# Modulation blocks released every 14000 of the planner's units instead of 4000, with 43 shared buffers and a 4096-byte scratch for dynamic DMA

## The chip, the core and the metric

The kernel runs on one core of a Trainium2 chip. The metric is the device time of one execution in microseconds (us). Work is spread over TensorE (PE, with its weight loads on PEld), VectorE (DVE), ScalarE (ACT), GpSimd (POOL), and the DMA queues, most of them issued from SyncE (SP). A measurement of this kernel spreads by about 0.1% either way, so a difference of 0.2% (6 us) is about the least that can be told from none.

## The reference

Two blocks on 1024 tokens and 256 context tokens, width 1024, all in float32:

```python
def hybrid_layer(x, xc, c_act, cc_act, w_mod, b_mod, w_in, ...):   # two layers
    shift, scale, gate = jnp.split(c_act @ w_mod + b_mod, 3, axis=-1)
    h = x * (1 + scale[:, None]) + shift[:, None]
    rk, rv, nk, nv, rq, rg, nq, ng, ch, cb, ccg, cz = split_cols(h @ w_in, PROJ_SPLITS)
    mod_c = jnp.split(cc_act @ w_mod[:, :n_mod * D_MODEL] + b_mod[:n_mod * D_MODEL], n_mod)
    hc = xc * (1 + mod_c[1]) + mod_c[0]          # the context, projected in the same way
    y_conv = short_conv_branch(...)              # 4 groups
    y_ret, yc_ret = retention_branch(...)        # 6 heads, chunks of 128, both directions
    y_na, yc_na = neighbourhood_branch(...)      # 6 heads, softmax over an 8x16 window and the context
    y = jnp.concatenate([y_conv, y_ret, y_na], axis=-1) @ w_out
    return layer_norm(ALPHA * x + gate[:, None] * y, ln_g, ln_b), ...
```

The second block takes the result through a gated delta rule (4 heads of 128, chunks of 64) beside dilated attention (8 heads of 64, three patterns), an output projection, and a gated feed-forward part of 2816 columns. What matters here is the first line of each layer: shift, scale and gate are products of one activated vector (c, and one of the context) with the 1024 x 3072 matrix `w_mod` of that layer. They depend on no token, so they can be computed at any time before the layer that uses them; the layer 1 values are not wanted before layer 0 has ended.

## The kernel before, in words

**Arithmetic.** A float32 operand is split into a high and a low part, and a projection is three matmuls, `xl*wh`, `xh*wh` and `xh*wl`, of 128 x 128 weights and up to 512 columns into one of 8 PSUM banks (`pb`). ScalarE makes `wh` and GpSimd makes `wl` from each loaded weight tile.

**Stages.** In the profiled execution: hidden states of layer 0 to 62 us; the V projection to 132; the retention pairs of layer 0 to 345; its conv, neighbourhood-attention (NA) and gate parts to 690; its output and layer norm to 865; layer 1 the same way to 1545 (V to 930, retention to 1110, then conv, NA and gates); the second block's V to 1605; the delta rule and the projections beside it to 1800; dilated attention to 2205; output to 2320; feed-forward to 2745; its last product to 3012.

**What sets the order.** TensorE runs its instructions in the order in which the Python emits them (`tc.manual_schedule`). That order comes from a planner, the class `Mixer`. It keeps a clock of its own, `vt`, and a list `active` of generators (softmax chains, retention chains, the modulation blocks), each with a due time. When a projection's matmul is emitted, `pe()` moves the clock and lets due generators take a step, so that their small matmuls are woven between projections: this text calls that **woven**. Two helpers do otherwise: `run_until(cond)` steps the generators one after the other, with no projection between, until `cond` holds. These stretches are called **forced** here. DVE, ACT, POOL and SP instructions are placed by priority, and the priority is the planner's time (`rank`); those of the modulation blocks get 5000 added (`late=X_MOD`).

**What sets a forced stretch off.** All large tiles come from one pool "S" of `NS` buffers of 4 KB per partition. `room()` counts free buffers, less what each active generator may still take: the larger of zero and its `peak` less what it holds. `S()` (an allocation outside a generator) forces steps until `room() >= 1 - over` with `over` = 2, `need_room(n)` until `room() >= n`, `need_o` and `need2` until a named pair is done. So a generator that stays alive holds room back from everything else.

**The modulation blocks.** `mods_gen` computes 32 blocks of 128 outputs: the last 8 of layer 0 and the 24 of layer 1 (the first 16 of layer 0 are done ahead, in the first stage). Per block it takes a buffer `wm`, loads 512 KB, yields, has DVE multiply and reduce it against `crow` (one or two reductions, named `mjk` and `wm` by where they write, each with a sum `macc`), makes `mod`, frees `wm`, and yields 4000. While it lives it holds the two `crow` buffers and `mjk`, and has a `peak` of 2 on top. It is added right after the hidden states, before the V projection.

**Order of the parts.** `ORDER1` is `r0 r1 r2 c0 n0 c1 n1 g0 g1 n2 g2 g3 g4 g5` in layer 0: three retention pairs, conv groups, NA pairs, gates. `ret_blocks`, `conv_blocks` and `gate_block` all allocate with `S()`; `n` is preceded by `need_room(9)`. The software DMA queue, issued by POOL, is used only at the start of each of the 6 NA pairs, for 11 transfers each (8 of them `nvr`).

Of the kernel before, what the change touches and what calls it, by code (L numbers as in the profile page):

```python
# [26 lines left out]
class Mixer:  # L27
# [7 lines left out]
    def __init__(self):  # L35
# [11 lines left out]
        self.banks = {}  # L47
        self.slots = [0.0] * Base.NS
        self.held = {}
# [213 lines left out]
class Base:  # L263
# [26 lines left out]
        self.uid += 1  # L290
        return f"{s}_{self.uid}"

    NS = 40
    OVER = {}
    NCS = 15

    def S(self, name, shape=(128, 1024), dt=F32):
# [4 lines left out]
        if self.mix.owner is None:  # L302
            self.mix.run_until(lambda: self.mix.room() >= 1 - self.mix.over)
        t = self.pm.tile(list(shape), dt, tag="S", bufs=self.NS, name=self.nm(name))
        self.mix.new_slot(self.mix.key(t))
# [177 lines left out]
class Layers(Base):  # L483
    X_RET = (1500, 1500)
    AHEAD = 3
    STEPS = 2
    X_MOD = 5000.0


    def setup(self):  # L490
# [54 lines left out]
    def mod_gen(self, l, blocks):  # L545
        for b in blocks:
            w = self.S("wm")
            self.nc.sync.dma_start(out=w, in_=self.io["w_modT"][l, b])
            yield
            self.mod_block(l, b, w, 1 if l == 1 and b >= 16 else 2)  # L550
            self.free(w)
            yield 4000
        if l:
            self.free(*self.crow, self.mjk)

# [1053 lines left out]
    def block1(self, stop=None):  # L1609
# [16 lines left out]
        def ready_k(k):  # L1626
            while steps[0] <= min(k + self.STEPS, 7):
                next(h0, None)
                steps[0] += 1
                if steps[0] == 8:  # L1630
                    mix.ratio = 10.0
                    mix.add(self.mods_gen(), True, peak=2, late=self.X_MOD)

# [1062 lines left out]
```

## Time and profile before

| | us |
|---|---|
| median of 3 runs (3010.87 to 3014.09) | 3012.46 |
| the profiled execution | 3013.66 |
| its span | 3011.9 |
| TensorE busy | 2734.6 (91%) |
| VectorE busy | 1986.3 (66%) |
| ScalarE / GpSimd busy | 1185.1 (39%) / 1168.4 (39%) |
| mean granted TensorE clock | 0.952 of full speed |

TensorE is the engine that decides: it is busy for 91% of the span, and the time it is not busy, with the time that it runs below its full clock, is what the order of the work can change. A stretch gives busy time and count per engine, the granted clock as a share of the full 2.4 GHz, the share of the DMA engines and GB/s. A row of waits says which engine and operation TensorE waited for, the total, the count and the longest.

### The profile page before, as it was taken

To read this page: it belongs to the slowest core of one execution; us is meant where nothing else is said; L and a number is where in the kernel's file an instruction comes from. 1 tells how busy PE (TensorE), PEld (TensorE's weight loads), DVE (VectorE), ACT (ScalarE), POOL (GpSimd) and SP (SyncE) were. 2 spreads that over 40 slices of the span, in tenths; PEclk is the share of its full clock that TensorE was granted. 3 is DMA by queue.
4 is the path that set the end of the run, shared out by engine and by line. 5 is a ranking of instruction groups with operands and counts; after the bars stand their busy time and mean duration, and the time that the engine had idled before them with its cause. 6 is when DMAs were issued, how large, how long until landed. Compare 5 with 4: busy or idle time off the path is not lost. (4 is left out here: it accounts for less than half of the span.)

```text
span 3011.9 us, 41163 instructions
## 1 busy us (share of the span) xinstructions
PE 2734.6 (91%) x14508; PEld 2339.8 (78%) x14508; DVE 1986.3 (66%) x3880; ACT 1185.1 (39%) x2691; POOL 1168.4 (39%) x998
## 2 busy tenths in 40 slices
PE   7989999999989989999889968898888899999888
PEld 6977888888778768887787767777767688888666
DVE  6666675684641567665555887777645777776786
ACT  5212254553442125554343323455544333334333
POOL 3345512213443451222563322111145644445755
PEclk9989999999989999999999979899999999999899
DMA  7533212225333221224444343221353222227244
GB/s 255 184 107 98 98 31 80 81 80 194 116 100 103 54 69 36 94 80 154 159 129 143 131 149 109 79 78 53 118 181 108 87 80 80 81 80 283 74 158 157
DMA packets 160975, 341.13 MB, mean 113 GB/s; under 512 B 28704, under 2 KB 56640, under 8 KB 160768
## 3 DMA queue, kind: packets, MB, share of 16 engines
q1 hardware_dynamic: 147968, 316.33, 31.1%
q10 hardware_dynamic: 10016, 13.12, 1.8%
q0 software_dynamic: 2784, 9.05, 1.0%
q8 instruction: 115, 1.88, 0.3%
q14 instruction: 92, 0.75, 0.1%
HBM read 265.46 MB, written 66.67 MB: 110 GB/s over the span
## 5 line engine op out<-in xcount | busy, mean ns | idle before, releaser
L251 POOL TENSOR_TENSOR wl<-wr,wh 128x512 fp32r<-128x512 f32 (+2 forms) x344 | 460.8, 1344 | 1142.3 <-ACT wh L251 1065.7
L344 PE MATMUL pb<-xh,wl 128*128 128x512 f32 x1456 | 579.9, 398 | 1.8 <-POOL wl L251 1.7
L344 PE MATMUL pb<-xh,wh 128*128 128x512 f32 x1456 | 578.9, 398 | 0.0
L344 PE MATMUL pb<-xl,wh 128*128 128x512 f32 x1456 | 578.4, 397 | 0.0
L251 ACT ACTIVATE wh<-wr 128x512 fp32r<-128x512 f32 (+2 forms) x344 | 203.0, 592 | 430.0 <-PE pb L344 328.2
L344 PEld LDWEIGHTS pb<-xh,wl 128*128 128x128 f32 x1456 | 277.4, 191 | 58.3 <-POOL wl L251 3.0
L344 PEld LDWEIGHTS pb<-xh,wh 128*128 128x128 f32 x1456 | 278.0, 191 | 53.4 <-issue 0.3
L344 PEld LDWEIGHTS pb<-xl,wh 128*128 128x128 f32 x1456 | 277.2, 190 | 54.0 <-issue 0.3
L344 PE MATMUL pb<-wh,yhl 128*128 128x512 f32 x832 | 266.4, 399 | 14.1 <-DVE xl L251 4.9
L344 PE MATMUL pb<-T,wh 128*128 128x512 f32 x640 | 198.1, 391 | 11.7 <-DVE T L251 10.4
L344 PEld LDWEIGHTS pb<-wh,yhl 128*128 128x128 f32 x832 | 159.7, 192 | 50.7 <-issue 8.0
L251 POOL TENSOR_TENSOR wl<-ws,wh 128x512 fp32r<-128x512 f32 x100 | 136.2, 1362 | 137.4 <-ACT wh L251 136.3
L344 PE MATMUL pb<-whi,yhl 128*128 128x512 f32 x528 | 174.5, 410 | 14.1 <-DVE yhl L251 6.1
L251 DVE TENSOR_TENSOR yhl<-yr,yhl 128x512 fp32r<-128x512 f32 (+4 forms) x122 | 116.4, 978 | 97.5 <-ACT yhl L251 93.6
L344 PE MATMUL pb<-wl,yhl 128*128 128x512 f32 x416 | 165.7, 398 | 7.3 <-POOL wl L251 7.3
L251 ACT ACTIVATE pt<-pb 128x512 fp32r<-128x512 f32 (+3 forms) x230 | 114.7, 527 | 122.9 <-PE pb L349 120.7
L251 DVE TENSOR_TENSOR pt<-pb,pt 128x512 fp32r<-128x512 f32 (+3 forms) x230 | 129.4, 596 | 49.7 <-ACT pt L251 49.0
L344 PEld LDWEIGHTS pb<-T,wh 128*128 128x128 f32 x640 | 120.5, 189 | 37.5 <-DVE T L251 10.9
L344 PEld LDWEIGHTS pb<-whi,yhl 128*128 128x128 f32 x528 | 104.9, 199 | 40.7 <-ACT whi L251 7.4
L344 PE MATMUL pb<-wl,xh 128*128 128x384 f32 (+1 forms) x384 | 127.4, 332 | 6.5 <-POOL wl L251 6.5
L251 ACT ACTIVATE wh<-ws 128x512 fp32r<-128x512 f32 x100 | 63.2, 632 | 169.8 <-PE pb L344 168.2
L344 PE MATMUL pb<-wh,xl 128*128 128x384 f32 (+1 forms) x384 | 126.4, 329 | 3.8 <-ACT wh L251 1.4
(435 smaller groups left out, 6188.7 us busy)
## 6 DMA issues: line engine op xcount, KB each, us to landing
wr<-in_w_in_dram SPq DMA_DIRECT2D x152, 256.0 KB, 2.7
ws<-in_w_down_dram SPq DMA_DIRECT2D x110, 256.0 KB, 3.8
wr<-in_w_out_dram SPq DMA_DIRECT2D x96, 256.0 KB, 2.9
wm<-in_w_modT_dram SPq DMA_DIRECT2D x32, 512.0 KB, 4.2
wr<-in_w_v_dram SPq DMA_DIRECT2D x64, 192.0 KB, 2.4
ws<-in_w_gate_dram SPq DMA_DIRECT2D x22, 512.0 KB, 5.2
ws<-in_w_up_dram SPq DMA_DIRECT2D x22, 512.0 KB, 4.8
ffn<-F SPq DMA_DIRECT2D x22, 512.0 KB, 3.0
```

The lines of the kernel that those rows point to most:

```text
L251: return fn(*a, **kw)
L344: self.mix.product(c / 2.4, out, (lhsT, rhs), lambda: self.nc.tensor.matmul(out, lhsT, rhs, start=start, stop=stop))
```

## The change

Three numbers: `NS` goes from 40 to 43, the modulation generator yields 14000 instead of 4000 after each block, and the compiled program reserves 4096 bytes for dynamic-DMA scratch, where the default stood before.

```diff
-    NS = 40
+    NS = 43
@@ class Layers
+    MOD_STEP = 14000.0
@@ def mod_gen
             self.mod_block(l, b, w, 1 if l == 1 and b >= 16 else 2)
             self.free(w)
-            yield 4000
+            yield self.MOD_STEP
@@ def kernel
-    nc = _bacc.Bacc("TRN2", target_bir_lowering=False, num_devices=1)
+    nc = _bacc.Bacc("TRN2", target_bir_lowering=False, num_devices=1, dynamic_dma_scratch_size=4096)
```

No instruction is added or taken away on TensorE (11891 rows in both orders). Through the planner the order changes in layer 0 between the first retention pair and the end of the third NA pair, at the end of the last but one NA pair of layer 1, and in the dilated stage. The scratch size alone leaves the order as it was.

First place: TensorE, the first retention pair. `vwc`, `vw`, `ktc`, `kt`, `q` and `k` are retention tiles, `xl`/`xh`/`wl`/`wh` a projection. Before:

```order
L344 MATMUL pb_1746<-ch_367,wh_1636 128x256
L344 MATMUL pb_1746<-ch_367,wl_1637 128x256
L344 MATMUL pb_1799<-vwc_1731,ktc_1716 64x128 x2
L344 MATMUL pb_1799<-vwc_1732,ktc_1716 64x128 x2
L344 MATMUL pb_1804<-vw_1721,kt_1703 64x128 x8
L344 MATMUL pb_1813<-vw_1726,kt_1703 64x128 x8
L344 MATMUL pb_1847<-q_1317,k_1316 128x128
L344 MATMUL pb_1848<-q_1317,k_1316 128x128
```

After, at the same row:

```order
L344 MATMUL pb_1696<-ch_367,wh_1588 128x256
L344 MATMUL pb_1696<-ch_367,wl_1589 128x256
L344 MATMUL pb_1738<-xl_189,wh_1594 128x512
L344 MATMUL pb_1738<-xh_187,wh_1594 128x512
L344 MATMUL pb_1738<-xh_187,wl_1595 128x512
L344 MATMUL pb_1738<-xl_189,wh_1594 128x512
```

The whole forced stretch of that pair (60 rows, the products of `vw`, `q`, `k`, `St`, `rv` and the transposes) is gone; its matmuls now stand woven among the projections that follow.

Second place: TensorE, the first NA pair of layer 0, at the end of its score products `kc*qc`; `sl` and `sc` are the softmax's rows, transposed through `ident`, and `pt`, `nv` the transposed weights and the values. Before:

```order
L344 MATMUL pb_3643<-kc_684_3333,qc_703_3452 128x256
L344 MATMUL pb_3643<-kc_684_3333,qc_705_3454 128x256
L344 MATMUL pb_3583<-xh_251,wh_3468 128x512
L344 MATMUL pb_3583<-xh_251,wl_3469 128x512
L344 MATMUL pb_3583<-xl_253,wh_3468 128x512
L344 MATMUL pb_3583<-xh_251,wh_3468 128x512
```

After:

```order
L344 MATMUL pb_3533<-kc_650_3239,qc_670_3360 128x256
L344 MATMUL pb_3533<-kc_650_3239,qc_672_3362 128x256
L349 MATMUL pb_3569<-ident,sl_3483 128x128 x4
L349 MATMUL pb_3577<-ident,sc_3484 128x128
L349 MATMUL pb_3577<-ident,sc_3485 128x128
L349 MATMUL pb_3577<-ident,sc_3484 128x128
```

Where projections stood between scores and transposes, the transposes now follow at once. The three NA pairs of layer 0 have such stretches of 150, 150 and 97 matmuls without a projection; before, the longest in them were 71 and 35.

Third place: TensorE in the dilated stage, where `dsl` is a softmax row and `dv` a value. Before:

```order
L349 MATMUL pb_19996<-ident,dsl_19887 128x128
L349 MATMUL pb_19996<-ident,dsl_19888 128x128
L344 MATMUL pb_20004<-pt_19962,dv_19857 128x256 x4
L344 MATMUL pb_20004<-pt_19969,dv_19857 128x256 x2
L344 MATMUL pb_20004<-pt_19969,dv_19857 128x128 x2
L344 MATMUL pb_20017<-pt_19977,dv_19857 128x256 x4
```

After, in the same part of the program:

```order
L344 MATMUL pb_20000<-xh_14758,wh_19604 128x512
L349 MATMUL pb_20019<-ident,dsl_19878 128x128
L349 MATMUL pb_20019<-ident,dsl_19879 128x128
L349 MATMUL pb_20019<-ident,dsl_19878 128x128
L349 MATMUL pb_20019<-ident,dsl_19879 128x128
L349 MATMUL pb_20027<-ident,dsl_19878 128x128
```

Before, this stage has stretches without projections of 276, 96, 116 and 96 matmuls. After, it has one of 279 and one of 88 at its end, and between them none longer than 30. On VectorE the 32 modulation blocks, all ahead of the first NA softmax before, are spread out: 16 of them now stand behind that softmax, 5 of these within the three long NA stretches (two, two and one).

## Rows read from the trace of the kernel before

**Rows 1.** The page: span and busy time of each engine.

```profile
span 3011.9 us, 41163 instructions
PE 2734.6 (91%) x14508; PEld 2339.8 (78%) x14508; DVE 1986.3 (66%) x3880; ACT 1185.1 (39%) x2691; POOL 1168.4 (39%) x998
```

**Rows 2.** Busy time by stage: stretch, length, engines (count), clock, DMA share, GB/s.

```profile
62.00:132.00 70.00, 66.82 (x372) 65.73 (x372) 52.15 (x99) 21.62 (x68) 34.34 (x26) 0.95 0.52 165
132.00:345.00 213.00, 194.15 (x1203) 165.54 (x1202) 147.11 (x357) 37.90 (x74) 108.30 (x96) 0.92 0.37 110
345.00:515.00 170.00, 167.59 (x989) 147.37 (x988) 105.64 (x270) 80.04 (x212) 49.14 (x59) 1.00 0.21 69
515.00:690.00 175.00, 166.06 (x1025) 149.09 (x1024) 126.97 (x349) 96.11 (x265) 26.94 (x29) 0.96 0.28 93
1800.00:2205.00 405.00, 351.63 (x2142) 301.91 (x2141) 292.26 (x782) 201.94 (x483) 65.35 (x58) 0.95 0.28 93
```

**Rows 3.** The same view: first retention pair, then woven retention of a later pair.

```profile
200.00:233.30 33.30, 21.09 (x161) 18.63 (x160) 31.14 (x71) 4.61 (x9) 18.62 (x17) 0.64 0.39 105
...
319.90:322.30 2.40, 2.40 (x42) 2.23 (x41) 2.40 (x4) 0.39 (x1) 1.28 (x3) 1.00 0.96 333
328.50:336.20 7.70, 7.70 (x76) 6.46 (x76) 6.80 (x22) 0.00 (x0) 1.73 (x4) 1.00 0.00 0
```

**Rows 4.** TensorE's waits from 200 to 233.3 us: total, times, longest.

```profile
PE pb L349 <- DVE k L251: 6.0, 1, 6.0
PE pb L344 <- DVE St L251: 4.9, 1, 4.9
```

**Rows 5.** Stretches: woven parts of the first NA pair of layer 0.

```profile
390.80:394.10 3.30, 3.16 (x22) 2.94 (x22) 2.14 (x7) 1.80 (x5) 1.04 (x1) 1.00 0.42 159
405.80:412.70 6.90, 6.90 (x58) 6.90 (x57) 4.95 (x12) 3.32 (x9) 1.28 (x1) 1.00 0.00 0
426.90:430.50 3.60, 3.60 (x28) 3.56 (x28) 2.51 (x9) 0.76 (x2) 0.00 (x0) 1.00 0.10 36
```

**Rows 6.** Stretches: forced NA parts, two of layer 0 and one of layer 1.

```profile
552.10:568.20 16.10, 11.32 (x74) 10.03 (x73) 14.22 (x33) 8.32 (x22) 9.65 (x14) 0.79 0.35 109
668.60:681.50 12.90, 9.08 (x54) 8.47 (x53) 9.43 (x25) 4.43 (x9) 2.38 (x2) 0.74 0.62 203
...
1269.00:1295.60 26.60, 19.50 (x117) 17.51 (x116) 21.98 (x57) 15.70 (x46) 10.92 (x15) 0.81 0.27 87
```

**Rows 7.** TensorE's waits from 1269 to 1295.6 us.

```profile
PE pb L349 <- DVE sl L251: 6.3, 4, 2.7
```

**Rows 8.** Tiles of the modulation blocks: ns min/median/max, first and last start.

```profile
L251 DVE CUSTOM_DVE_ANT_0 mjk<-wm,crow x24: 1204/1224/2332, 67.2 to 269.6; 128x1024 f32<-128x1024 f32 x24
...
L251 SPq DMA_DIRECT2D wm<-in_w_modT_dram x32: 327/384/702, 61.1 to 321.1; - x32
L251 DVE CUSTOM_DVE_ANT_0 wm<-wm,crow x32: 1208/1224/2306, 69.6 to 340.8; 128x1024 f32<-128x1024 f32 x32
...
L251 DVE TENSOR_SCALAR mod<-macc,bmod x40: 201/223/1310, 22.1 to 342.3; 128x2 f32<-128x2 f32 x32, 128x1 f32<-128x1 f32 x8
```

**Rows 9.** Stretches: three forced parts of the dilated stage.

```profile
2008.60:2027.20 18.60, 13.66 (x98) 11.87 (x97) 17.15 (x59) 12.21 (x28) 1.30 (x1) 1.00 0.18 54
2060.80:2089.70 28.90, 20.11 (x117) 17.81 (x118) 27.24 (x84) 17.04 (x37) 1.59 (x2) 0.88 0.08 26
2139.20:2159.90 20.70, 15.05 (x97) 13.16 (x98) 17.80 (x56) 12.26 (x29) 1.02 (x1) 0.92 0.30 95
```

**Rows 10.** TensorE's waits from 2060.8 to 2089.7 us.

```profile
PE pb L344 <- ACT dQ L251: 4.8, 1, 4.8
PE pb L349 <- DVE dsl L251: 3.6, 1, 3.6
```

**Rows 11.** The software queue on the page, and the tile `nvr`.

```profile
q0 software_dynamic: 2784, 9.05, 1.0%
L251 POOL DMA_DIRECT2D nvr<-nvd x48: 522/555/841, 358.9 to 1287.2; - x48
DMA to landing us min/median/max: 2.1/2.7/5.7
```

## The prediction

> **What bounds the kernel now.** The first view is the page's busy times: TensorE is busy for 2734.6 of 3011.9 us, VectorE for 66%, the others for 39% [rows 1]. TensorE does the same matmuls before and after, so the change can act only on the 277 us in which it is not busy and on the stretches at a lower clock. The second view, busy time by stage [rows 2], says where these lie. In 132–345 us TensorE stands for 18.9 us at a mean clock of 0.92; in 345–515 for only 2.4 us at full clock; in 515–690 for 9 us; in the dilated stage for 53 us. The third view goes into short stretches. Nearly all the loss of 132–345 lies in one, 200–233.3, the forced first retention pair: TensorE is busy for 21.1 of 33.3 us, at clock 0.64, while VectorE is busy for 31.1 [rows 3]. The waits there name VectorE's `k` (6.0 us) and `St` (4.9 us) [rows 4]. So: woven work runs at TensorE's rate, forced work at VectorE's rate, and the change shifts work between the two kinds.
>
> **The change, part by part.** The prices are two: what a matmul costs woven, and what it costs forced.
>
> *Retention pair 0 becomes woven.* The forced stretch held 161 matmuls of the trace. Woven, 42 of the small `vw*kt` kind took 2.40 us (0.057 each) and 76 of the others 7.70 us (0.101 each) [rows 3]. With 40 of the first and 121 of the second that is 2.3 + 12.3 = 14.6 us against 33.3, a gain of 18.7. It could be less, because the same VectorE work must still be done in the stage: VectorE is busy for 147 of 213 us [rows 2]. But about half of the modulation blocks leave the stage too. A block is one or two reductions of 1.22 us and a `mod` of 0.22, so 2.7 us with two [rows 8]. With some 16 of the 32 blocks gone, some 35 us, VectorE has 112 us in 194, 58%, which is less than the 62% and 73% of the two NA stretches where weaving works. I take 18.7; the bounds are 10, if one of the two long waits stays, and 24 (the whole 18.9 us of idle time, and some of the clock).
>
> *NA pairs of layer 0 become forced.* The price of woven NA: three stretches of the first pair have 22 + 58 + 28 = 108 matmuls in 3.3 + 6.9 + 3.6 = 13.8 us, 0.128 each [rows 5]. The price of forced NA: 74 in 16.1 and 117 in 26.6 us, 0.224 each [rows 6]; the waits there are for VectorE's `sl`, 6.3 us in four [rows 7], so the softmax chain sets the pace. The three new stretches have 150 + 150 + 97 = 397 matmuls: 89 us forced against 51 woven, +38. That has no modulation block in it. Five now stand in these stretches, two with two reductions and three with one, 2 x 2.7 + 3 x 1.4 = 9.7 us of VectorE time. In the forced rows VectorE works 36.2 of 42.7 us, 85% [rows 6], so for 397 matmuls 75 us; with the blocks 85 us, and at the same share 100 us, +49. The blocks are hidden in VectorE's idle 15% in the one case, and not at all in the other. I take the middle, +44. Below, the bound is 34 (85 us with VectorE never idle); above, 57: the slowest of the forced stretches is 28.9 us for 117 matmuls [rows 9], 0.247 each, so 98 us, and 9.7 for the blocks, against 51.
>
> The clock bears on this. The row of 200–233.3 has a clock of 0.64, so TensorE ran much of it at 1.2 and not 2.4 GHz, right where it waited [rows 3, 4]; the two shorter ones have 0.79 and 0.81 [rows 6]. The Trainium skill (TensorE: Matmul & The Clock Gate, Part 1: The HAM clock gate) calls the throttled clock the default that activity lifts; the trace agrees, with that 0.64. By the rule alone a stretch twice as long with more waits would stay at half the clock throughout: 19.5 us busy at 0.81 is some 0.135 us per matmul at the full clock and 0.27 at half, 107 us for 397, and +56 instead of +44. The row speaks for less: at 0.64 the retention stretch still took 33.3 / 161 = 0.207 per matmul, no more than those at 0.8, since VectorE was late in any case.
>
> *Forced pieces in layer 0 that go.* 552.1–568.2 took 16.1 us for 74 matmuls; woven 9.5, a gain of 6.6. At 668.6–681.5 the end of pair 2 no longer stands forced before the layer norm; its 12.9 − 9.1 = 3.8 us of waiting go [rows 6]. (The +44 was reckoned against all 397 woven, so these two count in full.) Together −10.4, between −4 and −13.
>
> *Less VectorE work while V is projected.* Of 62–132 us TensorE stands for 3.2 us, with VectorE busy for 52 of 70 [rows 2]. With blocks coming at twice to three times the interval I take −2, between 0 and −3.
>
> *End of layer 1's second pair.* 115 forced matmuls become 76: 39 x (0.227 − 0.128) = −3.9, from the 26.6 us for 117 [rows 5, 6]; between 0 and −5.
>
> *Dilated stage.* Three forced stretches of 98, 117 and 97 matmuls take 18.6 + 28.9 + 20.7 = 68.2 us, of which TensorE is busy for 48.8 [rows 9]: 19.4 us of waiting, for `dQ` and `dsl` among others [rows 10], and with clocks of 0.88 and 0.92 some 5 us lost to the clock. These 24 us are the most that weaving can give. One stretch of 88 matmuls remains, at the waiting of the first, 4.9 us per 98: 4.4. So up to −20. But VectorE is busy for 62.2 of those 68.2 us [rows 9] and for 72% of the whole stage [rows 2], and the new order still has pieces of 20 to 30 matmuls without a projection. I take −14, between 0 and −20. The long forced stretch at the start of the stage stays.
>
> *43 buffers, 4096 bytes of scratch.* The scratch moves no instruction. The buffers act only through the order, counted above; three more loads may start early, which costs nothing while DMA is busy for 21–37% of these stages [rows 2]. I take 0, within 2 us either way.
>
> *Sum:* −18.7 + 44 − 10.4 − 2 − 3.9 − 14 = −5.0 us. The profiled execution took 3013.66 (its span of 3011.9 and 1.8 around it), so 3008.7; it stood 1.2 above the median of the runs, so 3007.5 for the median. About 0.2% (6 us) is what a measurement of this kernel can tell from no change.
>
> **The rivals.**
>
> *More is won than lost.* If the blocks hide in VectorE's gaps (+38) and the dilated stage gives all 20, the sum is −5 − 6 − 6 = −17, 2995. For it: woven parts of layer 0 stand at clock 1.00 with 2.4 us idle in 170. Against it: VectorE's 91% in the dilated stretches.
>
> *The spread-out blocks hold up the softmax (slower).* Before, every block had ended by 342 us, ahead of the first NA pair [rows 8]. Now 16 stand behind its first softmax, and VectorE takes its work in order: a reduction ahead of a scaling of `sl` delays the transposes by 1.22 us, and the weights `pt` behind them. If the five in the forced stretches are paid in full (+49) and the other eleven by one reduction each (13 us), the sum is −5 + 5 + 13 = +13, 3025. It decides from where the forced stretches cost 49: no gain is left then, and from six of the eleven blocks on it is slower by more than 0.2%. For it: forced TensorE waits on `sl` [rows 7]. Against it: the eleven stand where projections are woven in, and there a late softmax costs TensorE nothing, as the 345–515 row shows with VectorE at 62%.
>
> *The scratch is too small.* Each NA pair issues 11 transfers on the software queue, 8 of them `nvr`, at 0.55 us each on POOL, landing after 2.7 us [rows 11]. If a smaller scratch let only one be under way, each pair's 11 would take some 30 us and not 6, 24 us later for each of 6 pairs. The loads are started just ahead of their pair, so much of the 144 us would show: I put 100, 3110. Against it: the whole queue moves 9 MB in 1.0% of the engines' time [rows 11]. The Trainium skill (DMA: Bandwidth & Descriptors, SWDGE vs HWDGE vs iDMA) says that these rings lie in a part of SBUF set aside for them; no run so far shows what a shorter one does.
>
> *The change does next to nothing* (3012): the order differs in hundreds of rows, but if VectorE sets the pace in both orders over layer 0 as a whole, forced and woven come to the same.
>
> **How the numbers follow.** The forecast, −5 with its own range of 2998 to 3016: 0.45 (faster by over 0.2% 0.20, within 0.23, slower 0.02). More won than lost: 0.24 (0.23 faster, 0.01 within). Blocks hold up the softmax: 0.24 (0.19 slower, 0.05 within). Scratch: 0.03, slower. Next to nothing: 0.04, within. That makes faster 0.43, within 0.33, slower 0.24. The range: the lower end takes the second case with the bounds of retention (−24), 2989; the upper end the third, 3026. The stall of the scratch and the outer halves of cases two and three are left out.
>
> **What would show it.** Right: 200–230 us without a stretch below clock 0.9, and the stage after V some 18 us shorter; three stretches in layer 0 after that with TensorE busy for 60–75%, waiting for `sl` and `pt`, of 32–36 us for 150 matmuls; the stage of 345–690 some 30 us longer; the dilated stage some 14 us shorter; layer 1 and the feed-forward part the same within 4 us. Wrong: NA stretches at 0.15 per matmul (faster than forecast) or at 0.27 (slower); woven parts of layer 0 with waits for VectorE just behind a `mjk` or `wm` reduction; `nvr` landing later than 6 us after its issue; or a dilated stage as long as before.

## The result and the profile after

The changed kernel takes 3036.7 us (median of 4 runs, 3030.5 to 3040.9) against 3013.3: a ratio of 1.007 (95% interval 1.0057 to 1.0082), which is some 21 us slower (the two medians are 23.5 us apart). The forecast was 3007.5 with a range of 2989 to 3026. Its profiled execution takes 3035.01 us, its span is 3033.2.

To see where the time went, the start of the same TensorE matmul (counted from the first; there are 14508 in every trace, and at each of these counts both orders have done the same matmuls) is compared in the two traces. The difference grows or shrinks stage by stage:

| matmul | before, us | after, us | difference | the stage since the row above: measured (forecast) |
|---|---|---|---|---|
| 200, start of the V projection | 62.9 | 61.0 | −1.9 | −1.9 (0) |
| 608, end of the V projection | 140.1 | 131.6 | −8.5 | V projection −6.6 (−2) |
| 2000, ahead of the first NA pair | 387.8 | 388.5 | +0.7 | retention +9.2 (−18.7) |
| 3720, end of layer 0's gates | 679.6 | 723.6 | +44.0 | NA +43.3 (+33.6: +44 − 10.4) |
| 6900, layer 1 after its second NA pair | 1307.3 | 1346.5 | +39.2 | −4.8 (−3.9) |
| 9300, start of the dilated stage | 1823.4 | 1860.4 | +37.0 | −2.2 (0) |
| 11300, end of the dilated stage | 2197.0 | 2214.5 | +17.4 | −19.6 (−14) |
| 13500, ahead of the last product | 2724.7 | 2742.3 | +17.6 | +0.2 (0) |
| 14507, the last | 3000.2 | 3022.8 | +22.6 | +5.0 (0) |

The last difference is 27.6 us above the forecast of −5.0. One stage, retention in layer 0, is 27.9 us above its own forecast, and the other misses, of either sign, cancel. It answers to [rows 2 to 4]. How far such a difference can be trusted shows in a run described below that has the order of the kernel before: its stages differ from that kernel's by 0.5 us in retention, 0.1 us in NA and 2.8 us in layer 1.

TensorE's waits in the retention stage, from matmul 608 to 2000 (line waited for, total, times, longest), first before and then after:

```profile
PE pb L349 <- DVE k L251: 9.9, 3, 6.0
PE pb L344 <- DVE St L251: 4.9, 1, 4.9
PE pb L349 <- POOL O L251: 3.4, 2, 2.1
PE pb L344 <- POOL wl L251: 1.7, 2, 1.3
```

```profile
PE pb L349 <- POOL O L251: 12.1, 2, 6.4
PE pb L344 <- POOL wl L251: 9.7, 4, 4.5
PE pb L349 <- DVE k L251: 2.2, 1, 2.2
```

VectorE's `k` and `St` have all but gone, as forecast. GpSimd's `O` and `wl` have come in their place: 21.8 us of waits for GpSimd where there were 5.1. In each of the four longest of them the clock falls to half, for 37.5 us in all (34.1 before). The same matmuls by busy time (stretch, length, engines, clock, DMA), before and after:

```profile
140.10:387.80 247.70, 227.55 (x1394) 192.72 (x1394) 166.34 (x401) 51.41 (x105) 126.13 (x122) 0.93 0.36 108
131.60:388.50 256.90, 232.77 (x1394) 194.36 (x1394) 153.68 (x363) 47.94 (x101) 124.78 (x122) 0.93 0.30 86
```

TensorE is idle for 24.1 us where it was 20.2, and busy for 5.2 us longer on the same 1394 matmuls, though VectorE now works for 153.7 us and not 166.3. What GpSimd did up to the first of the long waits (start, duration, operation; the wait runs from 222.0 to 227.7):

```profile
214.37 2.40 POOL L251 TENSOR_TENSOR k<-k,ropeC 128x1024 f32<-128x1024 f32 x1
216.73 1.29 POOL L251 TENSOR_TENSOR wl<-wr,wh 128x512 fp32r<-128x512 f32 x1
217.98 3.39 POOL L251 TENSOR_TENSOR q<-q,ropeC 128x1024 f32<-128x1024 f32 x1
221.46 1.05 POOL L251 TENSOR_SCALAR rsq<-va 128x8 f32<-128x8 f32 x1
222.59 2.31 POOL L251 TENSOR_TENSOR wl<-wr,wh 128x512 fp32r<-128x512 f32 x1
224.86 1.67 POOL L251 TENSOR_TENSOR rs<-rsq,mhalf 128x8 f32<-128x8 f32 x1
226.61 1.04 POOL L251 TENSOR_TENSOR O<-O,rs 128x512 f32<-128x512 f32 x1
```

The head norm of pair 0 (`rsq`, `rs`, `O`) stands behind the rotary products of pair 1 (`k*ropeC`, `q*ropeC`) and two weight splits. In the kernel before, with the pair forced, the same products and two splits stood ahead of it:

```profile
213.59 2.34 POOL L251 TENSOR_TENSOR k<-k,ropeC 128x1024 f32<-128x1024 f32 x1
217.15 2.50 POOL L251 TENSOR_TENSOR wl<-wr,wh 128x512 fp32r<-128x512 f32 x2
219.60 2.86 POOL L251 TENSOR_TENSOR q<-q,ropeC 128x1024 f32<-128x1024 f32 x1
224.23 1.09 POOL L251 TENSOR_SCALAR rsq<-va 128x8 f32<-128x8 f32 x1 [1.77 <-DVE va L251]
```

There GpSimd was through with them 1.8 us before VectorE delivered `va`, at 224.1, and TensorE itself stood waiting for VectorE's `k` until 225.4; it then waited only 1.3 us for `O`. In the changed kernel VectorE delivers `va` at 215.3, and GpSimd takes it up 6.2 us later. So weaving removed the wait for VectorE, and GpSimd's queue, hidden behind that wait before, became the next one to set the pace. For pair 1 it is a new queue: the second long wait (6.4 us, to 293.1) has the rotary products of pair 2 ahead of the head norm, and before they came behind it. The kernel before had the same wait where retention was already woven, in layer 1. From 1005 to 1200 us TensorE waited there for:

```profile
PE pb L349 <- POOL O L251: 13.6, 3, 6.8
```

The three forced NA stretches answer to [rows 6, 7]:

```profile
394.50:432.00 37.50, 27.26 (x151) 25.85 (x152) 31.75 (x97) 22.07 (x65) 1.28 (x1) 0.74 0.18 59
527.50:562.40 34.90, 24.03 (x151) 21.85 (x152) 29.39 (x93) 21.51 (x65) 1.37 (x2) 0.80 0.20 63
634.00:661.00 27.00, 15.50 (x95) 13.79 (x94) 21.23 (x73) 16.87 (x56) 1.28 (x1) 0.79 0.21 64
```

Together 99.4 us, 0.250 per matmul, with VectorE at 83%: the forecast was 95 (51 woven and 44 on top). In the first, 388.5 to 425 us:

```profile
PE pb L349 <- DVE sl L251: 10.0, 2, 5.4
PE pb L344 <- ACT q L251: 4.4, 1, 4.4
```

Two waits for the softmax, one per head, and one for ScalarE's `q` ahead of them, at 390.1 to 394.5. The `q` waits for VectorE, where a modulation block stands ahead of the low part of `q` (start, duration, operation):

```profile
384.85 1.23 DVE L251 CUSTOM_DVE_ANT_0 mjk<-wm,crow 128x1024 f32<-128x1024 f32 x1
387.00 1.23 DVE L251 CUSTOM_DVE_ANT_0 wm<-wm,crow 128x1024 f32<-128x1024 f32 x1
388.52 1.39 DVE L251 TENSOR_TENSOR q<-pb,q 64x512 fp32r<-64x512 f32 x2
```

A block stands in the first wait for the softmax too (VectorE, start, duration, operation):

```profile
400.98 0.16 DVE L251 TENSOR_SCALAR nmx<-mx 128x2 f32<-128x2 f32 x1
401.05 1.22 DVE L251 CUSTOM_DVE_ANT_0 mjk<-wm,crow 128x1024 f32<-128x1024 f32 x1
...
402.31 1.22 DVE L251 CUSTOM_DVE_ANT_0 wm<-wm,crow 128x1024 f32<-128x1024 f32 x1
...
403.90 0.35 DVE L251 TENSOR_SCALAR sl<-sl,rsm 128x256 f32<-128x256 f32 x1
```

The dilated stage, from the same matmul to the same matmul, first after and then before:

```profile
1860.40:2214.50 354.10, 323.22 (x2004) 279.44 (x2003) 268.11 (x735) 195.14 (x466) 55.73 (x51) 0.96 0.28 91
```

```profile
1823.40:2197.00 373.60, 327.44 (x2003) 281.95 (x2002) 269.76 (x735) 195.04 (x466) 55.91 (x51) 0.95 0.26 87
```

The same work is 19.5 us shorter: idle time of TensorE goes from 46.2 to 30.9 us, and its busy time from 327.4 to 323.2.

### The profile page after: what moved, and what is told of

It is laid out like the page before. It is cut to its first block, busy times and chain, and to the rows that moved or that the text cites. A ratio compares the mean times of both kernels' runs of the same rounds, so it can differ in the third digit from the quotient of the medians.

```text
span 3033.2 us, 41100 instructions
## 1 busy us (share of the span) xinstructions
PE 2739.6 (90%) x14508; PEld 2341.9 (77%) x14508; DVE 1979.0 (65%) x3880; ACT 1184.6 (39%) x2691; POOL 1163.9 (38%) x998
## 5 line engine op out<-in xcount | busy, mean ns | idle before, releaser
L344 PE MATMUL pb<-xh,wl 128*128 128x512 f32 x1456 | 581.1, 399 | 10.4 <-POOL wl L251 10.4
L344 PE MATMUL pb<-whi,yhl 128*128 128x512 f32 x528 | 174.5, 410 | 11.3 <-DVE yhl L251 6.0
L344 PE MATMUL pb<-wlo,yhl 128*128 128x512 f32 x264 | 110.1, 417 | 20.5 <-POOL wlo L251 20.4
```

The source lines that it names most:

```text
L344: self.mix.product(c / 2.4, out, (lhsT, rhs), lambda: self.nc.tensor.matmul(out, lhsT, rhs, start=start, stop=stop))
```

## The experiments

Ratios are to the kernel before, run beside each group on the same chip; its median was 3012.6, 3017.1 and 3015.9 us for the three groups. Stage differences are to the trace of the kernel before and counted as in the table above; retention is matmul 608 to 2000 and NA 2000 to 3720.

**Scratch alone.** `dynamic_dma_scratch_size=4096` added to the kernel before.

> 4096 bytes of scratch alone; the order is that of before on every engine. Theory A: no change, 3013 within 3 us. Rival (a shorter ring makes the software queue's transfers wait for each other): the nvr loads land later than 5.7 us at worst, and the time is 3020 or more.

Measured 3014.5, 1.0007 (0.9998 to 1.0017). The software queue's loads land as before [rows 11]:

```profile
DMA to landing us min/median/max: 2.0/2.7/5.9
```

The rival of the small scratch falls. In the changed kernel these loads took up to 6.6 us, past the 6 us that the prediction had named as a sign of it; but the longer interval with the default scratch (below) has 7.4, so the scratch is not what delays them.

**Buffers and scratch without the longer interval.**

```diff
-            yield self.MOD_STEP
+            yield 4000
```

> The change without the longer interval (43 buffers, 4096 bytes of scratch, blocks every 4000 as before). In its order the NA pairs of layer 0 are woven as before, the first retention pair is woven as in the changed kernel, and the dilated stage is the changed kernel's. Theory A (room: the blocks, alive for longer, hold room back, S() forces the NA pairs, and that costs the 43 us between 388 and 680 us; the retention stage gains nothing because GpSimd's O comes late; the dilated stage gains 20): NA back to 0, layer 1 -6, dilated -20, retention 0 to +6, so 2990 (2983 to 3000), faster than before. Theory B (the buffers or the scratch themselves slow layer 0): NA stage still 20 us or more over before, 3010 or more.

Measured 2994.0, 0.9945 (0.9931 to 0.996): faster than before. NA −1.2, layer 1's changed pair −5.9 (matmul 6000 to 6900), dilated −18.6; but retention +8.2, and the long waits there name GpSimd, as in the changed kernel:

```profile
PE pb L349 <- POOL O L251: 12.7, 2, 7.0
PE pb L344 <- POOL wl L251: 5.9, 1, 5.9
PE pb L349 <- POOL Oc L251: 5.1, 1, 5.1
```

So the longer interval is what costs, and the stage with the first retention pair woven loses time with it (+9.2) and without it.

**The longer interval alone.** `yield 14000` in the kernel before, 40 buffers.

> The longer interval alone (40 buffers, no scratch setting, blocks every 14000). Its order forces the first retention pair (122 matmuls) and 71 + 154 + 36 matmuls of NA in layer 0; the dilated stage is the changed kernel's. Theory A: 261 forced NA matmuls at the changed kernel's 43/397 = 0.11 us over woven are +28, dilated -20, early VectorE relief -4, retention -0 to +10: 3020 (3010 to 3030). Theory B (buffers or scratch): NA stage within 5 us of before, about 2990.

Measured 3024.9, 1.0038 (1.0024 to 1.0052). NA +39.0, where +28 was expected for the 261 matmuls of its three long stretches: the price per forced matmul does not carry over to this order, and what the other 11 us are stays open (20 of the blocks' 56 reductions stand in its NA stage). Dilated −18.6, with the changed kernel's order of TensorE, and the last product 0. The new dilated order thus comes without more buffers. Retention is +7.6: the first pair is forced here, in a stretch of 226 matmuls where the kernel before has 158.

**An interval of 8000.** `MOD_STEP = 8000.0` in the changed kernel; one NA pair forced.

> The change with an interval of 8000 in place of 14000. Its order forces one of the three NA pairs of layer 0 (154 matmuls); retention woven and dilated as in the changed kernel. Theory A: the cost of one forced pair, 43/397 x 154 = 17 us, on top of the kernel with 43 buffers and the interval 4000: about 3007 (2998 to 3015), with only the first NA pair longer. Theory C (the modulation blocks' own VectorE work beside the softmax is what costs, forced or not): all three pairs longer in proportion to the blocks that stand in them, most of all the first.

Measured 3012.4, 0.9993 (0.9982 to 1.0005). The first pair costs 21.7 us and the others 0. The expected time was 3007 and the first pair's cost 17. With 0, 1 and 3 forced pairs (intervals 4000, 8000, 14000) the NA stage costs −1, +20.5 and +43. This run alone does not tell the room theory from that of the blocks: all the blocks that it leaves in the NA stage stand before 479 us, that is in the first pair, the same that is forced. The next two runs part the two.

**Forced, with no block.** Interval 4000, and five more buffers of room demanded in the NA phases.

```diff
-    MOD_STEP = 14000.0
+    MOD_STEP = 4000.0
-    OVER = {}
+    OVER = {"na0.0": -3, "na0.1": -3, "na0.2": -3}
```

> 43 buffers, scratch 4096, interval 4000 (all blocks done before the first NA pair), but the planner is made to demand five more buffers of room during the three NA phases of layer 0, so that all three pairs are forced (154 matmuls each, 462 in all) with no modulation block among them. Room theory: forced work costs over woven what the forced rows of the kernel before gave, 0.224 - 0.128 = 0.096 us each, +44 on the 2994 of the kernel with interval 4000, so 3038 (3028 to 3045). Block theory (it is the blocks on VectorE that cost): NA within 10 us of woven, 3005 or less.

Measured 3031.2, 1.0054 (1.0039 to 1.0069). NA +35.1 without one block in it, and the waits in the first pair are the changed kernel's:

```profile
PE pb L349 <- DVE sl L251: 10.0, 2, 5.2
```

So forcing is the main cost of the NA stage: 35 of 43 us, or 30 if its 462 forced matmuls are scaled to the changed kernel's 397. That leaves 8 to 13 us, by subtraction, for the blocks, 5 of them in the first pair (17.0 against 22.2). The wait for `sl` with the block in it is no longer than without, but TensorE waits 0.5 us for ScalarE's `q` here and 4.4 us in the changed kernel.

**Blocks, but woven.** The changed kernel with its NA phases allowed to overdraw by two more buffers.

```diff
-    OVER = {}
+    OVER = {"na0.0": 4, "na0.1": 4, "na0.2": 4}
```

> The changed kernel (43 buffers, scratch 4096, interval 14000, blocks spread through the NA stage), but the planner may overdraw its room by two more buffers during the three NA phases of layer 0, so that the NA pairs are woven again; one forced stretch of 124 matmuls stands before the third pair. Room theory: NA +43 of the changed kernel falls to about +10 to +14 (124 x 0.096 = 12), so about 3005 (2998 to 3012). Block theory: at least +30 stays, 3023 or more.

Measured 3013.4, 0.9992 (0.9977 to 1.0006), 1.4 us above the expected range. NA +22.7 in place of +43.3: +7.7 in the first pair, woven but with blocks, and 11.3 around the forced stretch of 124. In the first pair TensorE waits 3.2 us for `q`, behind the same block as in the changed kernel. So the blocks are not free even in woven work; I had put that at nothing.

**42 buffers.** `NS = 42`, scratch 4096, interval 4000.

> 42 buffers, scratch 4096, interval 4000. Its order weaves the first retention pair, keeps the NA pairs woven, but has the old dilated stage with its three forced stretches (96, 116, 96). Theory: the 19 us of the dilated stage come from those three stretches alone, so 2994 + 19 = 3013 (3008 to 3018), with the dilated stage as long as before and the last product still 5 us longer. Rival (the buffers themselves make the dilated stage faster): about 2997.

Measured 3028.5, 1.0034 (1.0019 to 1.005), above the expected range. The dilated stage is as expected, +1.2 with the old order of three forced stretches, so the 19 us of that stage belong to its order and not to the number of buffers. The miss is in retention, +16.7, woven again. Its waits for GpSimd are those of the run with 43 buffers and interval 4000 (26.1 us against 25.9), but the clock is at half for 47.8 us of the stage where that run has 34.1. The two orders of TensorE differ there in only 37 places, so differences of some 8 us between woven versions of this stage say little about their order.

**Rotary products on VectorE, interval 4000, 43 buffers.**

```diff
-            self.tt(t, t, self.ropeC, ALU.mult, nc.gpsimd)
+            self.tt(t, t, self.ropeC, ALU.mult)
```

> The kernel with 43 buffers, scratch 4096, interval 4000, with the rotary products k*cos and q*cos of the retention pairs (both layers) on VectorE and not on GpSimd. Theory: the waits for GpSimd's O and Oc (7.0 + 5.7 + 5.1 us) and for wl behind them (5.9) in the retention stage of layer 0 come from GpSimd's queue, where the two products of 2.4 us or more stand ahead of the head norm; most of them go, the retention stage is 10 us or more shorter, 2984 (2975 to 2990). Rival: O is late for its own slow operations (the power and the scaling, some 3.5 us), or VectorE's k comes as much later: no gain, 2990 to 2998.

Measured 2982.3, 0.989 (0.9875 to 0.9904). Retention −6.6, from +8.2, with the order of TensorE unchanged up to layer 1. The wait for `O` goes from 12.7 to 3.7 us:

```profile
PE pb L344 <- POOL vw L251: 4.4, 3, 3.8
PE pb L349 <- POOL O L251: 3.7, 3, 1.7
PE pb L349 <- POOL Oc L251: 3.6, 1, 3.6
```

**The same edit in the changed kernel.**

> The changed kernel as it is (43 buffers, scratch 4096, interval 14000) with the rotary products k*cos and q*cos on VectorE. Theory: the retention stage of layer 0 gave nothing because GpSimd's O and wl came late; with its queue relieved, that stage ends 10 to 14 us earlier against the kernel before (at the last of its matmuls +1 becomes about -11), layer 1 gains 5 more, and the NA stage keeps its +43: 3022 (3015 to 3027). Rival (the stage is held by VectorE's total work, to which the products add): retention within 4 us of the changed kernel, 3030 or more.

Measured 3011.1, 0.9985 (0.9974 to 0.9995), better than expected. Retention is −11.2, where it was +9.2, with the same order of TensorE: 20.4 us come back by taking two products per pair out of GpSimd's queue. NA stays at +40.4.

**The same edit in the kernel before.**

> The kernel before (40 buffers, interval 4000, default scratch) with the same two products on VectorE; the first retention pair stays forced. Theory: forced, VectorE is what holds the pair, and GpSimd was late by only 3.4 us there; so 0 to 4 us in layer 0, and 5 in layer 1 where O was late: 3006 (3001 to 3011). If the woven first pair is worth something of its own once GpSimd is relieved, the kernel with 43 buffers and the products moved (2982) should be under this by more than the 18 us of the dilated stage. Rival: as much is gained here as with 43 buffers (12 us), 3001 or less.

Measured 3003.1, 0.9955 (0.9939 to 0.9971). Retention −4.0 with the first pair still forced; woven at the same interval it was −6.6. This is the control for the run before. Without the two products on GpSimd the change is worth −11.2 + 4.0 = −7.2 us in retention; with them it is +9.2. So 16.4 of the 27.9 us that the forecast missed there belong to these products in GpSimd's queue; the other 4.0 of the 20.4 are gained in the old order too.

**GpSimd relieved further.** Interval 4000, 43 buffers, rotary products on VectorE, and half of `vw` on ScalarE.

```diff
-                    self.ts(t[:, :, h, fb, :], V[:, 4 * b:4 * b + 4, 64 * h:64 * h + 64],
-                            wk[:, 2 * p + h, fb, :], None, ALU.mult, eng=nc.gpsimd if fb else None)
+                    o_, i_, w_ = t[:, :, h, fb, :], V[:, 4 * b:4 * b + 4, 64 * h:64 * h + 64], wk[:, 2 * p + h, fb, :]
+                    if fb:
+                        self.act(o_, i_, scale=w_)
+                    else:
+                        self.ts(o_, i_, w_, None, ALU.mult)
```

> 43 buffers, scratch 4096, interval 4000, rotary products on VectorE, and the backward half of vw (24 products of 128x256 by a column in each layer, GpSimd's before) on ScalarE, which is busy for some 15% of the retention stage. Theory (GpSimd's queue is what is left): the waits for vw (3.8 us) and Oc (3.6 us) go, 5 to 8 us less in layer 0 and a little in layer 1: 2975 (2969 to 2981). Rival (VectorE or the order now holds the stage): 2980 to 2986.

Measured 2957.4, 0.9802 (0.9778 to 0.9826), some 2% faster than the kernel before, and by more than expected: retention −15.2 in layer 0, −17.1 in layer 1 from matmul 3720 to 6900 (−7.0 with the rotary products alone), and the dilated stage's −18.9 as in the others. It is the fastest version of all, and it beats both kernels. The edit also moves TensorE's order in layer 0's retention (399 places against the run with the rotary products alone), so its gain there is not GpSimd's queue by itself; the waits for GpSimd fall from 13.4 to 7.7 us. TensorE, 132 to 345 us:

```profile
132.00:345.00 213.00, 205.29 (x1300) 174.28 (x1299) 161.19 (x390) 45.32 (x98) 91.62 (x93) 0.96 0.39 116
```

## Why the prediction was wrong

**The step that failed: "Retention pair 0 becomes woven", −18.7, measured +9.2.** The price was taken from two stretches of a later pair in which TensorE was never idle [rows 3], that is from the good parts of woven retention alone. Whether another engine could keep that pace was reckoned for VectorE ("58%") and not for GpSimd. GpSimd showed up in the same row, busy for 108 of 213 us [rows 2], and its `O` was waited for, up to 6.8 us a time, in layer 1's woven stage. The bound ("10, if one of the two long waits stays") allowed only the old waits to stay and no new one. The runs show the new one by name (waits for GpSimd from 5.1 to 21.8 us) and by removal: with the two products off GpSimd's queue the change gains 7.2 us in this stage instead of losing 9.2. That is still 11.5 us short of the forecast. In that run TensorE still waits 14.4 us for GpSimd in the stage; how much of the 11.5 these waits make up was not tested.

Whether weaving by itself can gain is not settled. Retention against before, from matmul 608 to 2000, with 43 buffers in the woven rows and 40 in the forced ones:

| first pair | blocks every | GpSimd | us |
|---|---|---|---|
| forced | 4000 | as before | 0 |
| woven | 4000 | as before | +8.2 |
| forced, a longer stretch | 14000 | as before | +7.6 |
| woven | 14000 | as before | +9.2 |
| forced | 4000 | without rotary products | −4.0 |
| woven | 4000 | without rotary products | −6.6 |
| woven | 14000 | without rotary products | −11.2 |
| woven | 4000 | without rotary products and half of `vw` | −15.2 |

As long as GpSimd keeps its work, weaving gains in neither pair of rows; with GpSimd relieved it gains 2.6 us at interval 4000, less than the runs with 42 and with 43 buffers lie apart in this stage (8.5 us). A forced pair at 14000 with GpSimd relieved was not run, so how much of the −11.2 is weaving, and how much the smaller number of blocks in the stage, stays open.

**NA pairs forced, +44, less 10.4 for pieces that go.** The mechanism was right, and the term nearly so: 99.4 us and not 95 for the 397 matmuls. The sum of the two was 9.7 us short. 4.4 of it is the long stretches being dearer. The rest lies outside them: waits for ScalarE's `q` just ahead of the first and the third (4.4 and 2.5 us), which no forced row of before had, and the blocks in the woven parts, which cost 7.7 us in the first pair when it was woven; the wait for `q` is part of either. The clock stayed at 0.74 to 0.80, so these longer stretches did not run at half the clock throughout, as the prediction had feared: they idle in waits of 5 us and are busy between them. The prediction had read that fear out of the Trainium skill (TensorE: Matmul & The Clock Gate, Part 1: The HAM clock gate), which calls the throttled clock the default that activity lifts; with these rows it agrees in so far as the clock fell in the waits and rose again in the work behind them.

**Blocks that hold up the softmax**, the slower rival, gave a time near the measured one for another reason. It asked 24 us of the blocks (11 in the forced stretches, +49 in place of +38, and 13 in the woven parts), and retention was to gain as in the forecast. The runs leave the blocks 8 to 13 us, against 30 to 35 for forcing, and its 13 in woven parts were 7.7 in the one pair where this could be seen. There the block held up `q`, ahead of the scores, as well as the softmax. That the range's upper end lies near the result is luck.

**Dilated stage, −14, measured −19.6.** Right in kind. The bound of −20 was the better estimate: it had nothing for the pieces of 20 to 30 matmuls without a projection. **Layer 1** (−3.9 against −4.8) was right in kind, though the run with the order of before differs by as much as 2.8 us there. The **V projection** (−2, at most −3, against −6.6) was right in kind and too small: TensorE no longer stands at all, but its clock rises too, from 0.95 to 1.00 [rows 2], and for that the term had nothing:

```profile
62.00:132.00 70.00, 70.00 (x405) 69.96 (x404) 31.74 (x69) 23.06 (x71) 32.24 (x28) 1.00 0.40 122
```

**The last product, 0, measured +5.0.** Every kernel with 43 buffers has it (4.7 to 5.0), those with 40 and 42 do not (−0.1 to 0.9), and TensorE's order there is the same in all. Its waits for GpSimd's `wlo` in that stage, before and then after:

```profile
PE pb L344 <- POOL wlo L251: 14.2, 12, 3.0
```

```profile
PE pb L344 <- POOL wlo L251: 20.4, 16, 4.3
```

In the kernel with 43 buffers and interval 4000, GpSimd takes `s` ahead of `wlo` at several places where it took them the other way round before. How three more buffers bring that about stays open; I had looked at the order of this stage on TensorE alone.

## What to carry to other kernels

When work is moved from a stretch of its own into the shade of other work, price it for every engine that the two have in common, and take the price from a whole stage that already runs so, its waits included, not from its best stretches. A stretch that looks wasteful because one engine is late may hide a second engine that is nearly as late: here it was GpSimd, 1.8 us ahead of VectorE. Room that a slow background task holds back is paid by whoever asks next: ask what its longer life takes from the allocator, not only what it takes from its engine.

## What the runs showed of the hardware

- A rotary product of 128x1024 on GpSimd took 2.3 to 3.5 us (median 2.4 for `k`, 2.6 for `q`, in the kernel before) and on VectorE 1.2 to 2.3 us (median 1.2 and 1.5, in the changed kernel with the products moved). The power in `rs` on 128x8 took 1.6 to 2.5 us on GpSimd in the kernel before. VectorE's reductions of 128x1024 took 1.2 us mostly and 2.3 at most [rows 8]. What stretches the longer ones no run isolates.
- A wait of 4.9 us in a forced NA stretch (idle from 531.2 to 536.0) came with 6.8 us at half the clock (from 533.4 to 540.2), 4.2 us of them behind the wait. Work at half the clock takes up to twice as long, so by these numbers such a wait costs TensorE up to some 2 us more than its length (an estimate).
- A scratch of 4096 bytes for dynamic DMA changed nothing that the traces show, with 11 transfers issued at a time: loads landed after 2.7 us in the median and 5.9 at most, against 2.7 and 5.7.
